# An RMSNorm kernel: the first early store on ScalarE's queue cut from four rows per partition to one, the second grown from four to seven

## The chip, the core and the metric

The kernel runs on one core of a Trainium2 chip. The core has five engines that work side by side: TensorE (PE) for matrix products, VectorE (DVE), ScalarE (ACT) and GpSimd (POOL) for elementwise work and reductions, and SyncE (SP), which here only issues DMA transfers. Transfers between the chip's memory and the 128 partitions of the on-chip memory are carried out by 16 DMA engines. SP and ACT each have a queue of their own that feeds the same 16 DMA engines: the profile calls SP's queue q1 and ACT's queue q10. The metric is the device time of one execution in microseconds (us), as the median over runs.

## The reference

```python
def reference(x, gamma):          # x: 16 x 1024 x 512 fp32, gamma: 512 fp32
    eps = 1e-5
    rms = np.sqrt(np.mean(x ** 2, axis=-1, keepdims=True) + eps)
    return (x / rms * gamma).astype(np.float32)
```

Every row of 512 numbers is divided by its root mean square and multiplied by gamma. The input is 16384 rows, 33.55 MB, and the output is as large.

## The kernel before

The 16384 rows are cut into four tiles t = 0 to 3, each of 128 partitions with 32 rows (R) of 512 fp32 numbers. One row of one partition is 2048 bytes; one row on all partitions is 256 KB, and a whole tile 8 MB. Three slots of on-chip memory hold a tile each; tile 3 uses slot 0 again, once tile 0 has been stored from it (`slot_of`, line 87).

The order of the work is written out by hand. `load` (line 44) always issues on SP's queue. `store` (line 48) issues on SP's queue unless another is named. In every transfer, a run of r rows of one partition is contiguous in both memories, so that a transfer is 128 packets of r x 2048 bytes, 8 for each of the 16 DMA engines.

The work on the engines goes by `groups` (line 76): tile, first row, number of rows, how the rows are cut for the square sums, and how many rows at the end of the group are POOL's share. For each group, ACT squares the rows and DVE sums them (`square_sums`, lines 96 and 97), ACT takes the root and DVE the reciprocal (`inverse_rms`, lines 102 and 103). Then POOL scales its share and multiplies it by gamma (lines 109 and 110), ACT scales the other rows one at a time (line 118), and DVE multiplies these by gamma in one instruction (`times_gamma`, line 122). The square sums of the next group are issued ahead of this group's scaling. All results are written in place, into the slot.

Tile 0 has three groups: rows 0 to 6 (rows 0 to 3 by ACT and DVE, rows 4 to 6 by POOL), rows 7 to 15 (7 to 10 by ACT and DVE, 11 to 15 by POOL), and rows 16 to 31. The first eight rows of tile 0 are stored from ACT's queue, in two pieces: one is issued while the group at row 7 is worked on (line 173), the other while the group at row 16 is (line 179). A third such piece is rows 0 to 3 of tile 1 (line 181). All other stores, and all loads, are issued by SP in a fixed order (`transfers`, line 129): among others the store of tile 0's rows 8 to 15 and 16 to 31, then the loads of tile 2's rows 23 to 31 and of tile 3 into slot 0. The load of tile 3's rows 0 to 15 overwrites the rows that the two pieces on ACT's queue, and the store of rows 8 to 15, have read, so SP waits for these three before it issues that load.

Of the kernel before, what the change touches and what calls it, by code (L numbers as in the profile page):

```python
# [9 lines left out]
def kernel(  # L10
# [6 lines left out]
    nc = tc.nc  # L17
# [30 lines left out]
    def store(t, slot, r0, r1, queue=nc.sync):  # L48
        dma = queue.dma_start(out=ov[t][:, r0:r1], in_=slots[slot][:, r0:r1])  # L49
        before_scale.append((slot, r0, r1, dma))  # L50
# [38 lines left out]
    def square_sums(ss, t, g, r, m, k):  # L89
        if m == 9:  # L90
            sq = slots[2][:, 23:32, :]
        else:
            home, name, most = ((psum, "sq_psum", 7), (const, "sq_sbuf", 5))[k % 2]
            sq = home.tile([P, most, D], fp32, name=name)
        rows = slots[slot_of[t]][:, g + r : g + r + m, :]
        nc.scalar.activation(out=sq[:, :m], in_=rows, func=AF.Square)  # L96
        nc.vector.tensor_reduce(  # L97
            out=ss[:, r : r + m, 0], in_=sq[:, :m], axis=mybir.AxisListType.X, op=OP.add
        )

    def inverse_rms(ss, n):
        nc.scalar.activation(out=ss[:, :n, 0], in_=ss[:, :n, 0], func=AF.Sqrt, bias=eps_t, scale=1.0 / D)  # L102
        nc.vector.reciprocal(out=ss[:, :n, 0], in_=ss[:, :n, 0])  # L103
        return ss

    def scale_by_pool(rstd, t, g, n, share):
        part = slots[slot_of[t]][:, g + n - share : g + n, :]
        by_row = rstd[:, n - share : n].to_broadcast([P, share, D])
        nc.gpsimd.tensor_tensor(out=part, in0=part, in1=by_row, op=OP.mult)  # L109
        last = nc.gpsimd.tensor_tensor(  # L110
            out=part, in0=part, in1=gamma_b.to_broadcast([P, share, D]), op=OP.mult
        )
        before_scale.append((slot_of[t], g + n - share, g + n, last))

    def scale(rstd, t, g, r0, r1):
        x = slots[slot_of[t]]
        for r in range(r0, r1):
            nc.scalar.activation(out=x[:, g + r, :], in_=x[:, g + r, :], func=AF.Copy, scale=rstd[:, r])  # L118

    def times_gamma(t, g, r0, r1):  # L120
        part = slots[slot_of[t]][:, g + r0 : g + r1, :]
        scaled = nc.vector.tensor_tensor(  # L122
            out=part, in0=part, in1=gamma_psum.to_broadcast([P, r1 - r0, D]), op=OP.mult
        )
        for slot, b0, b1, earlier in before_scale:
            if slot == slot_of[t] and b0 < g + r1 and g + r0 < b1:
                tc.declare_no_dep(scaled.ins, earlier.ins, reason="ScalarE waited for it before it scaled these rows")

    def transfers(t, g):
        if (t, g) == (0, 0):  # L130
            load(1, 1, 16, 32)
            load(2, 2, 0, 23)
        elif (t, g) == (0, 16):
            store(0, 0, 8, 16)
            store(0, 0, 16, 32)
            load(2, 2, 23, 32)
            load(3, 0, 0, 16)
            load(3, 0, 16, 32)
        elif (t, g) == (1, 16):
            store(1, 1, 4, 32)  # L140
        elif (t, g) == (2, 16):
            store(2, 2, 0, 32)
        elif (t, g) == (3, 0):
            store(3, 0, 0, 16)
        elif (t, g) == (3, 16):
            store(3, 0, 16, 32)

    def pieces_of(group):
        t, g, n, pieces, share = group
        ss = stats.tile([P, 16, 1], fp32, name="ss")  # L150
        r = 0
        todo = []
        for k, m in enumerate(pieces):
            todo.append((ss, t, g, r, m, k))
            r += m
        return ss, todo
# [6 lines left out]
    for k, group in enumerate(groups):  # L163
        t, g, n, pieces, share = group
        mine = n - share
        half = (mine + 1) // 2
        ahead = groups[k + 1 :][:1]
        ss, todo = pieces_of(ahead[0]) if ahead else (None, [])
        scale_by_pool(rstd, t, g, n, share)
        for piece in todo[:2]:  # L170
            square_sums(*piece)
        if (t, g) == (0, 7):
            store(0, 0, 0, 4, nc.scalar)
        scale(rstd, t, g, 0, half)
        for piece in todo[2:]:
            square_sums(*piece)
        scale(rstd, t, g, half, mine)
        if (t, g) == (0, 16):
            store(0, 0, 4, 8, nc.scalar)
        elif (t, g) == (2, 0):  # L180
            store(1, 1, 0, 4, nc.scalar)
        times_gamma(t, g, 0, mine)
        transfers(t, g)
        for nxt in ahead:
            rstd = inverse_rms(ss, nxt[2])
# [30 lines left out]
```

## Time and profile before

| what | value |
|---|---|
| median of 3 runs | 161.56 us (161.45 to 161.64) |
| the profiled execution | 161.69 us, its span 159.8 us |
| DVE, ACT, POOL busy | 112.0, 107.8, 106.4 us |
| moved by DMA | 67.12 MB, 420 GB/s over the span |
| packets of q1 (SP) and q10 (ACT), share of 16 engines | 93.5% and 4.7% |
| last instruction of DVE (line 122) | from 132.10, 7.09 us long |
| issue of the two pieces on ACT's queue | 27.41 and 40.02 us |

The span is what the profiler saw of the program; the execution's own time contains 1.89 us around it. A time in the trace counts from the start of the span. "q1" and "q10" are SP's and ACT's DMA queues; "SPq" and "ACTq" are the sequencers that issue on them. A DMA share of 1 means that all 16 DMA engines were busy; over short stretches it can lie above 1, because a packet is counted in the stretch in which it begins. Beside the page and its views, the trace holds a record of every DMA packet (when it began, how long it took, its size, its queue) and of every step of a semaphore by which a transfer reports that it has landed; the single packet times and landing times in this document are from these records.

### The profile page before, as it was taken

How to read it: one execution, taken by the hardware profiler on the slowest of the kernel's cores; microseconds unless marked ns; L12 is line 12 of the kernel's file. 1: busy time of each engine (PE TensorE's matmuls, PEld its weight loads, DVE VectorE, ACT ScalarE, POOL GpSimd, SP SyncE). 2: the span in 40 equal slices, each digit the busy share in tenths (PEclk: the TensorE clock that was granted, in tenths of full speed). 3: DMA queues.
4: the chain of work that ended last, by engine and by line, in shares of the span. 5: the costliest groups of instructions: out<-in, count | busy, mean ns of one | idle time of the engine just before them, and what ended most of it. 6: DMA issues, size and time to landing. Idle time of an engine off the chain costs nothing.

```text
span 159.8 us, 273 instructions
## 1 busy us (share of the span) xinstructions
PE 2.0 (1%) x2; PEld 0.5 (0%) x2; DVE 112.0 (70%) x39; ACT 107.8 (67%) x108; POOL 106.4 (67%) x24
## 2 busy tenths in 40 slices
PE   0050000000000000000000000000000000000000
PEld 0010000000000000000000000000000000000000
DVE  0019098899798999999999999999999009800000
ACT  3071966975999999999899999989970990000000
POOL 1000960994999599999999999999999990000000
DMA  5999999999999998998999999999996997999995
GB/s 179 431 427 468 443 418 410 377 449 408 455 476 443 443 410 365 423 500 370 434 468 394 470 445 390 501 459 459 459 476 279 525 476 312 394 468 451 394 435 222
DMA packets 2747, 67.12 MB, mean 420 GB/s; under 512 B 313, under 2 KB 314, under 8 KB 442
## 3 DMA queue, kind: packets, MB, share of 16 engines
q1 hardware_dynamic: 2314, 63.97, 93.5%
q10 hardware_dynamic: 432, 3.15, 4.7%
q14 instruction: 1, 0.01, 0.0%
HBM read 33.56 MB, written 33.55 MB: 420 GB/s over the span
## 4 chain that ended last, share of the span: by engine, by line
DVE 59%; ACT 21%; DMA 4%; issue 1%; ACTq 1%; SPq 0%
DVE ss L97 36%; DVE slot L122 23%; ACT slot L118 8%; ACT slot L96 8%; ACT sq_psum L96 5%; DMA slot<-in_x_dram 4%; DVE ss L103 1%; ACT ss L102 0%; ACTq L211 0%; ACT gamma_b L162 0%; SPq L45 0%; ACTq L49 0%; ACTq L96 0%
## 5 line engine op out<-in xcount | busy, mean ns | idle before, releaser
L109 POOL TENSOR_TENSOR slot<-slot,ss 128x3584 f32<-128x3584 f32 (+2 forms) x9 | 46.9, 5213 | 24.2 <-DVE ss L103 24.2
L110 POOL TENSOR_TENSOR slot<-slot,gamma_b 128x3584 f32<-128x3584 f32 (+2 forms) x9 | 59.2, 6582 | 0.7
L97 DVE TENSOR_REDUCE ss<-sq_psum 128x7 f32<-128x3584 f32 (+1 forms) x13 | 42.2, 3245 | 13.7 <-ACT sq_psum L96 13.7
L118 ACT ACTIVATE slot<-slot,ss 128x512 f32<-128x512 f32 x75 | 47.2, 706 | 4.7 <-DVE ss L103 4.7
L122 DVE TENSOR_TENSOR slot<-slot,gamma_psum 128x4608 f32<-128x4608 f32 (+2 forms) x9 | 41.3, 4589 | 8.7 <-ACT slot L118 8.7
L96 ACT ACTIVATE sq_psum<-slot 128x3584 f32<-128x3584 f32 (+1 forms) x13 | 34.5, 2657 | 6.3 <-DMA slot<-in_x_dram 5.7
L97 DVE TENSOR_REDUCE ss<-slot 128x9 f32<-128x4608 f32 x3 | 14.9, 4954 | 4.4 <-ACT slot L96 4.2
L97 DVE TENSOR_REDUCE ss<-sq_sbuf 128x5 f32<-128x2560 f32 x5 | 14.0, 2800 | 0.0
L96 ACT ACTIVATE slot<-slot 128x4608 f32<-128x4608 f32 x3 | 12.1, 4032 | 0.0
L96 ACT ACTIVATE sq_sbuf<-slot 128x2560 f32<-128x2560 f32 x5 | 11.6, 2324 | 0.3 <-DMA slot<-in_x_dram 0.3
L102 ACT ACTIVATE ss<-ss,eps_t 128x16 f32<-128x16 f32 (+2 forms) x9 | 2.7, 304 | 11.7 <-DVE ss L97 11.7
L103 DVE RECIPROCAL ss<-ss 128x16 f32<-128x16 f32 (+2 forms) x9 | 2.1, 235 | 0.4 <-ACT ss L102 0.4
L66 PE MATMUL gamma_psum<-gamma_row,ones_col 1*128 1x512 f32 x2 | 2.0, 1122 | 8.7 <-DMA gamma_row<-in_gamma_dram 8.7
L72 ACT ACT_TABLE_LOAD x1 | 1.3, 1283 | 1.2 <-PEq L200 1.2
L162 ACT COPY gamma_b<-gamma_psum 128x512 f32<-128x512 f32 x1 | 0.6, 564 | 0.0
L66 PEld LDWEIGHTS gamma_psum<-gamma_row,ones_col 1*128 1x128 f32 x2 | 0.5, 305 | 8.6 <-issue 8.6
L64 POOL MEMSET ones_col<- 1x128 f32 x1 | 0.2, 194 | 0.3 <-POOLq L200 0.3
L200 POOL MEMSET const-float32-0.0<- 128x1 f32 x1 | 0.1, 98 | 0.2 <-issue 0.2
L72 ACT ACTIVATE table<-eps_t 128x1 f32<-128x1 f32 x1 | 0.2, 202 | 0.0
L200 POOL MEMSET const-bfloat16-1.0<- 128x1 bf16 x1 | 0.1, 101 | 0.0
L200 POOL MEMSET const-uint8-127<- 128x1 uint8 x1 | 0.1, 101 | 0.0
L200 POOL MEMSET const-float32-1.0<- 128x1 f32 x1 | 0.1, 98 | 0.0
(1 smaller groups left out, 0.1 us busy)
## 6 DMA issues: line engine op xcount, KB each, us to landing
slot<-in_x_dram SPq DMA_DIRECT2D x5, 4096.0 KB, 25.0
out_dram<-slot SPq DMA_DIRECT2D x3, 4096.0 KB, 20.2
out_dram<-slot SPq DMA_DIRECT2D x1, 7168.0 KB
slot<-in_x_dram SPq DMA_DIRECT2D x1, 5888.0 KB
out_dram<-slot ACTq DMA_DIRECT2D x3, 1024.0 KB
slot<-in_x_dram SPq DMA_DIRECT2D x1, 2304.0 KB, 25.7
slot<-in_x_dram SPq DMA_DIRECT2D x1, 2048.0 KB, 10.0
out_dram<-slot SPq DMA_DIRECT2D x1, 2048.0 KB
```

Of the source, the lines that this page charges most:

```text
L66: nc.tensor.matmul(gamma_psum[:, 0], ones_col, gamma_row, start=True, stop=True)
L72: nc.scalar.activation(out=table, in_=eps_t, func=AF.Sqrt)
L96: nc.scalar.activation(out=sq[:, :m], in_=rows, func=AF.Square)
L97: nc.vector.tensor_reduce(out=ss[:, r : r + m, 0], in_=sq[:, :m], axis=mybir.AxisListType.X, op=OP.add)
L102: nc.scalar.activation(out=ss[:, :n, 0], in_=ss[:, :n, 0], func=AF.Sqrt, bias=eps_t, scale=1.0 / D)
L103: nc.vector.reciprocal(out=ss[:, :n, 0], in_=ss[:, :n, 0])
L109: nc.gpsimd.tensor_tensor(out=part, in0=part, in1=by_row, op=OP.mult)
L110: last = nc.gpsimd.tensor_tensor(out=part, in0=part, in1=gamma_b.to_broadcast([P, share, D]), op=OP.mult)
L118: nc.scalar.activation(out=x[:, g + r, :], in_=x[:, g + r, :], func=AF.Copy, scale=rstd[:, r])
L122: scaled = nc.vector.tensor_tensor(out=part, in0=part, in1=gamma_psum.to_broadcast([P, r1 - r0, D]), op=OP.mult)
L162: nc.scalar.copy(out=gamma_b[:, 0], in_=gamma_psum[:, 0])
L200: nc = _bacc.Bacc("TRN2", target_bir_lowering=False, num_devices=1)
```

## The change

The first piece on ACT's queue is row 0 of tile 0 instead of rows 0 to 3. The second is rows 1 to 7 instead of rows 4 to 7. The places in the program at which they are issued stay the same.

```diff
         if (t, g) == (0, 7):
-            store(0, 0, 0, 4, nc.scalar)
+            store(0, 0, 0, 1, nc.scalar)
         scale(rstd, t, g, 0, half)
         for piece in todo[2:]:
             square_sums(*piece)
         scale(rstd, t, g, half, mine)
         if (t, g) == (0, 16):
-            store(0, 0, 4, 8, nc.scalar)
+            store(0, 0, 1, 8, nc.scalar)
         elif (t, g) == (2, 0):
             store(1, 1, 0, 4, nc.scalar)
```

## The prediction

> **What bounds the kernel now.** I read the page's head and its DMA rows first, then the chain that ended last, then a table of busy times by stretch, then the waits of SP's queue, then the timeline around the two stores. The page first:
>
> ```profile
> span 159.8 us, 273 instructions
> ...
> DMA  5999999999999998998999999999996997999995
> ...
> q1 hardware_dynamic: 2314, 63.97, 93.5%
> q10 hardware_dynamic: 432, 3.15, 4.7%
> ```
>
> The two queues' packets take 93.5% + 4.7% = 98.2% of the time of 16 DMA engines: 0.982 x 159.8 = 156.9 us. In the packet records the first packet of the kernel's loads begins at 1.76 us and the last one ends at 158.56. 1.76 + 156.8 = 158.6, so from the first packet to the last there is no gap on the DMA engines. The rest is the last landing (158.92), 0.8 us to the end of the span, and 1.9 us around it.
>
> The chain of waits seems to say something else. Its end:
>
> ```profile
> 125.95 6.13 ACT slot L118 x10
> 132.08 0.02 issue
> 132.10 7.09 DVE slot L122
> ```
>
> It follows the engines to 139.2 us, where DVE's last instruction ends, and stops there. But the last store, issued then, has its first packet at 148.35: 9.1 us behind older packets in q1. A queue that is empty needs about 1.0 us from issue to packet (SP's first issue at 0.74, first packet at 1.76). So the engines could be some 8.1 us later (148.35 - 1.0 - 139.2) before a DMA engine ran dry. The engines don't set the end; the packets do. The table by stretch (columns: stretch, its length, busy time of PE, PEld, DVE, ACT, POOL, clock, DMA share, GB/s):
>
> ```profile
> 4.00:20.00 16.00, 2.04 (x2) 0.49 (x2) 4.09 (x2) 7.67 (x4) 3.82 (x2) 1.00 1.04 445
> 20.00:28.00 8.00, 0.00 (x0) 0.00 (x0) 7.27 (x3) 5.43 (x7) 2.78 (x2) 1.00 0.97 418
> 28.00:34.00 6.00, 0.00 (x0) 0.00 (x0) 5.32 (x2) 6.00 (x5) 5.92 (x2) 1.00 0.95 371
> 34.00:44.00 10.00, 0.00 (x0) 0.00 (x0) 8.93 (x4) 7.43 (x5) 7.77 (x2) 1.00 1.03 442
> 44.00:62.00 18.00, 0.00 (x0) 0.00 (x0) 17.37 (x7) 17.64 (x21) 16.22 (x4) 1.00 1.00 429
> 62.00:90.00 28.00, 0.00 (x0) 0.00 (x0) 28.00 (x12) 26.45 (x28) 27.84 (x5) 1.00 1.01 436
> 104.00:139.20 35.20, 0.00 (x0) 0.00 (x0) 27.05 (x9) 22.14 (x29) 27.68 (x5) 1.00 1.01 436
> 139.20:150.00 10.80, 0.00 (x0) 0.00 (x0) 0.00 (x0) 0.00 (x0) 0.00 (x0) 1.00 1.00 434
> ```
>
> The DMA share is about 1 everywhere, at 418 to 445 GB/s, except from 28 to 34 us: busy, but 371 GB/s. There the packets are stretched: 31 packets of 32 KB that begin between 29.0 and 31.3 take up to 1.687 us instead of 1.213, together 0.52 us for each engine. It is the one loss in the middle of the run.
>
> **The change, part by part.** These lines of the timeline are the two issues and what stands around them, and the first reader of the load that the second store runs beside:
>
> ```profile
> 25.10 2.28 DVE L122 TENSOR_TENSOR slot<-slot,gamma_psum 128x2048 f32<-128x2048 f32 x1
> 27.41 0.38 ACTq L49 DMA_DIRECT2D out_dram<-slot  x1
> 40.02 0.34 ACTq L49 DMA_DIRECT2D out_dram<-slot  x1
> 64.45 3.14 ACT L96 ACTIVATE sq_psum<-slot 128x3584 f32<-128x3584 f32 x1
> ```
>
> *The issues.* The first store waits for DVE's one instruction over rows 0 to 3 (25.10 + 2.28 = 27.38), and row 0 alone needs the same instruction. The second waits for POOL's rows 4 to 6 and for row 7, which DVE ends at 39.72; rows 1 to 3 are ready since 27.38. Both are still 128 packets, so I take 0.38 and 0.34 us of ACTq for the issues as before. No issue moves: 0.
>
> *The packets, one engine's eight of each store.* In the records an 8192-byte packet of q10 takes 0.309 us, a 14336-byte one (first seen as a load of seven rows) 0.535, a 2048-byte one (the load of row 0) 0.084. First store: 8 x 0.309 = 2.47 us before, 8 x 0.084 = 0.67 after, 1.80 less. Second: 2.47 before, 8 x 0.535 = 4.28 after, 1.81 more. Sum: +0.01 us. Since the DMA engines have no gap, all of it would be on the path. The durations are of loads; no store of these sizes is shown. Bounds for a 2048-byte store packet: below, the bytes alone at the slope between 8192 and 32768 bytes ((1.213 - 0.309) / 24576 x 2048 = 0.075 us, a gain of 0.07 us for eight); above, the longest 2048-byte packet of the run, 0.667 us at its start (4.7 us for eight). For 14336 bytes: 0.527 by the same slope below (-0.06 us), 0.998 above (+3.7 us). I take the medians, 0.084 and 0.535, because the line through 8192 and 32768 bytes goes through both, and because 8192-byte stores lie on the line of the loads.
>
> *A rule against it.* The Trainium skill, "DMA: Bandwidth & Descriptors", section Bandwidth, advises transfers of at least 1 MiB, since each carries about 2.0 us that don't grow with its size; the first store falls to 256 KB. By its fit (2.0 us + bytes / 436 GB/s, given for another issue path) an estimate is 2.6 + 6.2 us for the new pair against 4.4 + 4.4 for the old, the same sum. Here nothing waits for that fixed part: between issue and first packet of the first store (27.8 to 31.98 us) the engines move loads.
>
> *The loads beside them.* Packets of the two queues alternate one by one: the first store's groups come every 1.515 us (1.213 + 0.309). With smaller packets in between, the load of tile 1's rows 16 to 31 lands 1.8 us sooner (45.3 to about 43.5); its reader starts at 50.49 behind DVE, so nothing is gained. The load of tile 2's rows 0 to 22 then starts 1.8 us sooner, has 1.8 us more of store packets between its own, and lands where it did, 61.3; its reader, the last line above, starts at 64.45 and has 3.1 us to spare. From there on q1 stands where it stood before: 0.
>
> *Who waits for the stores.* SP's own waits:
>
> ```profile
> SPq L45 <- DMA out_dram<-slot: 19.5, 3, 9.5
> SPq L211 <- DMA out_dram<-slot: 19.1, 2, 9.6
> ```
>
> The load of tile 3's rows 0 to 15 waits for both pieces and for the store of rows 8 to 15. The last landing is that store's, at 66.2. The second piece landed at 59.6; with 1.8 us more it lands near 61.4, 4.8 us before SP could go on. Behind SP's wait stand the load of rows 16 to 31 and the later stores, and q1 then holds packets until about 81. On ACT one wait moves: in tile 3 the scaling of row 1, not of row 4, now checks the second piece, at 97 us; it passed long ago: 0.
>
> *Sum.* +0.01 us on the profiled 161.69 us, which lies 0.13 above the median of 161.56. Forecast: 161.57 us.
>
> **Rivals.**
>
> *Faster: the loss at 29 to 32 us shrinks with the first store.* The stretched packets begin 1.2 us after the first store's issue ends and stop as its packets begin. If the loss is work done for that store by its bytes, a quarter of the bytes leaves a quarter of 0.52 us: -0.39, so 161.18 us; at most -0.52, 161.05. Against it: no packet of the store runs then, the second and third store of the same size (40.02 and 86.70) show nothing of the kind, and the first loads of q1 were stretched likewise (0.6 us for each engine from 1.8 to 7 us). That looks like the first use of a queue, whatever its size. 128 packets are set up either way.
>
> *Slower: the new packets cost what they did at the start of the run.* There, the 2048-byte packets took 0.117 us on average, the 14336-byte ones 0.572. If such packets don't follow on each other at full rate when they change places with long loads, 8 x 0.033 + 8 x 0.037 = 0.56 us come on top: 162.13 us. It decides from about 0.32 us, that is, 0.040 us for each of the eight small packets alone. For it: nothing in the run shows short store packets between long loads. Against it: the 8192-byte ones in that place cost 0.309 throughout, nothing over the line.
>
> *Slower: the second store lands too late.* SP would have to be held up from 66.3 until past some 80 us before q1 ran dry; the store would have to land 18 us later than I work out. Then each further microsecond is one on the time, 162.6 for one. Nothing speaks for it.
>
> *Faster by earlier loads.* That needs an engine that waits for the load which lands at 45.3 and an end set by the engines; neither is so. It gives 161.57, the forecast.
>
> **How the numbers follow.** The forecast, with the rival that gives the same time, has 0.64. The lost stretch shrinking has 0.14, and 0.02 goes to gains in the same place that I can't name: faster 0.16. The dearer packets have 0.17, the late second store or another hold-up of the queue 0.03: slower 0.20. Within 0.2% (0.32 us, about what a measurement of this kernel can tell from no change) is 161.24 to 161.88. The range goes down to the shrunken loss, 161.15, and up past the dearer packets, 162.2; it leaves out a loss that vanishes whole and a price of packets nearer to its upper bound, together about 0.12. The forecast's own range is 161.4 to 161.75, the runs' spread and a little more.
>
> **What would show it.** Right: q10's packets in two groups, eight per engine of about 0.084 us from about 32 us and eight of about 0.535 from about 44 us; DMA share near 1 from 2 to 158 us; the same dip at 28 to 34 us; tile 1's second load landing near 43.5; all instructions from 64 us on where they were. Wrong: a dip that is gone or smaller (the first rival), packets of q10 or the loads between them that take longer than these medians (the second), a gap in q1 (the third). The forecast fails where the time of the packets depends on their order and not only on their number and size.

## The result: slower, and scattered

| | before | changed |
|---|---|---|
| median of 8 runs | 161.61 us (161.45 to 161.78) | 162.63 us (161.94 to 163.59) |
| ratio | | 1.0063, 95% interval 1.0040 to 1.0086 |
| the profiled execution | 161.69 us, span 159.8 | 163.59 us, span 161.7 |

The changed kernel is slower by 0.6%, outside the forecast range, and its runs lie 1.65 us apart where those of the kernel before lie 0.33 apart. (A ratio here is not the quotient of the two medians beside it; with scattered runs the two differ by up to 0.3%.) The profiled execution of the changed kernel is the slowest of its eight, so that it shows the loss large.

The head and the DMA rows of the changed kernel's page:

```profile
span 161.7 us, 273 instructions
...
DMA  5999999999979979999999989999799969899990
...
q1 hardware_dynamic: 2314, 63.97, 92.5%
q10 hardware_dynamic: 432, 3.15, 4.6%
```

(92.5% + 4.6%) of 161.7 us is 157.0 us of packets, where the kernel before had 156.9. The average engine has no more to do, and 1.9 us of the span are new. The table by stretch shows where they are (columns as in the prediction; the last two are DMA share and GB/s). The kernel before, at the old dip and at its end:

```profile
28.00:34.00 6.00, 0.00 (x0) 0.00 (x0) 5.32 (x2) 6.00 (x5) 5.92 (x2) 1.00 0.95 371
40.00:52.00 12.00, 0.00 (x0) 0.00 (x0) 10.42 (x3) 12.00 (x13) 11.92 (x2) 1.00 1.06 457
56.00:60.00 4.00, 0.00 (x0) 0.00 (x0) 4.00 (x2) 3.64 (x6) 4.00 (x1) 1.00 0.95 410
158.00:159.00 1.00, 0.00 (x0) 0.00 (x0) 0.00 (x0) 0.00 (x0) 0.00 (x0) 1.00 0.01 0
159.00:160.00 1.00, 0.00 (x0) 0.00 (x0) 0.00 (x0) 0.00 (x0) 0.00 (x0) 1.00 0.00 0
```

The changed kernel, the same stretches:

```profile
28.00:34.00 6.00, 0.00 (x0) 0.00 (x0) 5.56 (x2) 6.00 (x5) 5.92 (x2) 1.00 0.98 421
40.00:52.00 12.00, 0.00 (x0) 0.00 (x0) 10.67 (x3) 12.00 (x13) 11.92 (x2) 1.00 1.04 433
56.00:60.00 4.00, 0.00 (x0) 0.00 (x0) 4.00 (x2) 3.64 (x6) 4.00 (x1) 1.00 0.89 367
158.00:159.00 1.00, 0.00 (x0) 0.00 (x0) 0.00 (x0) 0.00 (x0) 0.00 (x0) 1.00 0.08 33
159.00:160.00 1.00, 0.00 (x0) 0.00 (x0) 0.00 (x0) 0.00 (x0) 0.00 (x0) 1.00 0.08 33
```

Two things are to be seen. First, the dip at 28 to 34 us is gone (371 to 421 GB/s), and slower stretches have come at 40 to 52 and 56 to 60 us instead. By the packet records, the excess of all packets over the straight line of size between 24 and 60 us is 0.55 us for each engine before and 0.59 after: the loss moved and kept its size. In the profiles of all the kernels below this sum lies between 0.49 and 0.75 us, whatever the pieces; only its place changes. Second, from 158 to 160 us the changed kernel shows a DMA share of 0.08 and 33 GB/s: that is about one engine of 16, with one 32 KB packet in each microsecond. In the packet records, 15 of the 16 engines end between 158.01 and 158.61 us, where all 16 ended before (158.03 to 158.56). The last one ends at 160.50. In this profile, this engine alone is the 1.9 us.

When it fell behind is written in the landings. A transfer has landed when all 16 engines have done their share; the last engine comes after the median one by 0.28 us in the landing at 66.3 us, then by 0.58 (76.5), 1.08 (82.2), 1.44 (92.7) and 2.22 (105.2), and by as much to the end. Four packets lie on these steps: a 32 KB store packet at 74.1 us that took 2.09 us instead of 1.21, an 18 KB load packet at 76.2 (0.91 instead of 0.69), and 32 KB load packets at 90.7 (1.34) and 101.4 (2.29). The other packets of these sizes at 74 and 76 us took the usual time to 0.01 us. The records don't name the engine of a packet, so that these four are one engine's follows from the times alone. The lag stays to the end: no other engine takes over a part of the late engine's packets.

On the engines' side the delay shows above all as this wait. The kernel before:

```profile
ACT sq_sbuf L96 <- DMA slot<-in_x_dram: 0.3, 1, 0.3
```

The changed kernel:

```profile
ACT sq_sbuf L96 <- DMA slot<-in_x_dram: 1.3, 1, 1.3
```

It isn't the price: DVE's last instruction starts at 132.62 instead of 132.10 us, and the last store's packets begin at 148.4 in both.

### The profile page after: what moved, and what is told of

The parts are those of the page before. It is cut to its first block, busy times and chain, and to the rows that moved or that the text cites. A ratio compares the mean times of both kernels' runs of the same rounds, so it can differ in the third digit from the quotient of the medians.

```text
span 161.7 us, 273 instructions
## 1 busy us (share of the span) xinstructions
PE 2.0 (1%) x2; PEld 0.5 (0%) x2; DVE 112.2 (69%) x39; ACT 107.7 (67%) x108; POOL 106.4 (66%) x24
## 3 DMA queue, kind: packets, MB, share of 16 engines
q1 hardware_dynamic: 2314, 63.97, 92.5%
## 4 chain that ended last, share of the span: by engine, by line
DVE 36%; ACT 27%; DMA 21%; issue 1%; ACTq 1%; SPq 0%
DMA slot<-in_x_dram 21%; DVE ss L97 19%; DVE slot L122 17%; ACT slot L118 11%; ACT slot L96 7%; ACT sq_psum L96 6%; ACT sq_sbuf L96 1%; ACT ss L102 0%; ACTq L211 0%; DVE ss L103 0%; ACT gamma_b L162 0%; SPq L45 0%; SPq L49 0%; ACTq L49 0%; ACTq L96 0%
```

## The experiments

All ratios are to the kernel before, run beside on the same chip. "Dip" is the excess of the packets that begin from 28 to 34 us over the straight line of size, in us for each engine. Each dip comes from the one execution that was profiled. None of the runs of the kernel before that stood beside these was above 162.43 us, so runs of 163 us and more are counted. The experiments ran on four chips: the first four kernels of the table on one, two_six, no_first, four_singles and after_moved on a second, few_parts, before_moved and the two oneway kernels on a third, the two with `nudge` on a fourth. The changed kernel itself was not run beside the kernels on the third and the fourth.

| kernel | first store, then second | median (range), us | ratio (95%) | dip | runs from 163 us |
|---|---|---|---|---|---|
| changed, again | 1 row, 7 rows | 163.28 (161.63 to 164.06) | 1.0078 (1.0050 to 1.0105) | 0 | 8 of 12 |
| small_first | 1, 4 (3 by SP) | 162.10 (161.71 to 163.41) | 1.0041 (1.0018 to 1.0064) | 0 | 3 of 12 |
| large_second | 4, 7 | 161.79 (161.56 to 162.40) | 1.0005 (0.9992 to 1.0019) | 0.42 | 0 of 12 |
| swap | 7, 1 | 162.14 (161.74 to 162.61) | 1.0025 (1.0012 to 1.0037) | 0.74 | 0 of 12 |
| two_six | 2, 6 | 161.79 (161.48 to 163.36) | 1.0020 (1.0001 to 1.0039) | 0.06 | 1 of 12 |
| no_first | none, 8 | 162.72 (162.57 to 164.18) | 1.0096 (1.0066 to 1.0125) | 0 | 2 of 6 |
| four_singles | 4 x 1 row, 4 | 164.56 (164.48 to 164.73) | 1.0184 (1.0171 to 1.0197) | 0.02 | 4 of 4 |
| few_parts | 4 rows of 32 partitions, the rest | 161.95 (161.72 to 162.37) | 1.0026 (1.0017 to 1.0034) | 0.37 | 0 of 11 |
| after_moved | 1, 7, other order on q1 | 162.58 (161.71 to 164.06) | 1.0068 (1.0037 to 1.0100) | 0 | 6 of 12 |
| before_moved | 4, 4, other order on q1 | 162.03 (161.72 to 162.36) | 1.0027 (1.0017 to 1.0038) | 0.56 | 0 of 11 |
| oneway_before | 4, 4, no late loads | 161.46 (161.30 to 161.89) | 0.9991 (0.9980 to 1.0002) | 0.40 | 0 of 11 |
| oneway_after | 1, 7, no late loads | 161.46 (161.33 to 161.70) | 0.9991 (0.9982 to 1.0000) | 0 | 0 of 11 |
| after_nudge | 8 KB packets, then 1, 7 | 163.85 (163.12 to 164.46) | 1.0140 (1.0116 to 1.0164) | 0.25 | 6 of 6 |
| no_first_nudge | 8 KB packets, then none, 8 | 162.67 (162.04 to 163.99) | 1.0073 (1.0046 to 1.0100) | 0.26 | 4 of 12 |

### Which of the two pieces: the changed kernel again, and each part alone

The changed kernel again, without an edit:

> The changed kernel a second time, to see which part of its profile comes back. Theory A (the seven-row packets of the second store slow the loads they change places with): again about 1.006 of the kernel before, with stretched packets of the load of tile 2's rows 0 to 22 between 42 and 59 us, together about 0.4 us for each of the 16 DMA engines. Theory B (the small first store): the same time, and the dip at 29 to 32 us gone again. Theory C (one DMA engine falls behind the other 15 by chance, at places far from the two stores): fifteen engines end near 158.5 us again and one later, but the long packets of that one lie elsewhere than at 74 and 101 us, and the lag is 0.5 to 2 us.

The first piece alone:

```diff
-            store(0, 0, 0, 4, nc.scalar)
+            store(0, 0, 0, 1, nc.scalar)
...
         elif (t, g) == (0, 16):
+            store(0, 0, 1, 4)
             store(0, 0, 8, 16)
```

> Only the first piece made small: row 0 on ScalarE's queue, rows 1 to 3 go to SyncE's queue ahead of rows 8 to 15, and the second piece stays rows 4 to 7. Theory A: no loss, 0.998 to 1.001 of the kernel before. Theory B: the loss stays, 1.004 to 1.009. Theory C doesn't say which piece matters: a scatter of runs of 0.5 us or more if the small piece is what lets one engine fall behind, 0.2 us if not.

The second piece alone:

```diff
-            store(0, 0, 8, 16)
+            store(0, 0, 11, 16)
...
-            store(0, 0, 4, 8, nc.scalar)
+            store(0, 0, 4, 11, nc.scalar)
```

> Only the second piece made large: the first stays rows 0 to 3, the second is rows 4 to 10, and SyncE's store begins at row 11. Theory A: the loss is there, 1.004 to 1.009, with stretched load packets between 44 and 60 us. Theory B: 0.999 to 1.001, with the dip at 29 to 32 us as before the change. Theory C: a scatter of runs of 0.5 us or more if the large piece is what lets one engine fall behind.

The sizes the other way round:

```diff
-            store(0, 0, 0, 4, nc.scalar)
+            store(0, 0, 0, 7, nc.scalar)
...
-            store(0, 0, 4, 8, nc.scalar)
+            store(0, 0, 7, 8, nc.scalar)
```

> The sizes the other way round: first piece rows 0 to 6, second row 7. Theory A (the large piece costs where it stands beside loads): a loss between 32 and 46 us, 1.003 to 1.009. Theory B (a small first piece costs): no loss, 0.999 to 1.001, or a gain. Theory C: one late engine only if unequal pieces as such bring it, 1.003 to 1.01.

Measured: the loss and the scatter came back in the changed kernel. In this profile four engines were late, not one: twelve end by 158.75 us, the others at 159.70, 159.81, 160.14 and 160.16. The end of the span shows them, with a DMA share of 0.31 after 158 us, where the kernel before had 0.01:

```profile
156.00:158.00 2.00, 0.00 (x0) 0.00 (x0) 0.00 (x0) 0.00 (x0) 0.00 (x0) 1.00 0.99 426
158.00:159.00 1.00, 0.00 (x0) 0.00 (x0) 0.00 (x0) 0.00 (x0) 0.00 (x0) 1.00 0.31 131
```

Their long packets began at 74.1 to 74.3, 76.2 to 76.3, 89.0 to 89.5 and 101.3 to 101.9 us: the number of late engines changed from run to run, the places did not. So theory C's "by chance" holds for which engines and how many, and is wrong for where.

The large second store alone costs nothing that can be measured (+0.05%, interval from -0.08 to +0.19); theory A falls. The stretched loads that it forecast between 42 and 59 us did come in the changed kernel (0.64 us for each engine in this profile), but they came in place of the dip and not on top of it. The small first store alone costs 0.41%, with three runs at 163 us. The first piece is the one that matters. The changed kernel's 0.78% with the large second behind it is higher, but the two intervals overlap, so that the second makes it worse is likely and not shown. In the profile of small_first, itself a quick run of 161.97 us, no engine is late. The swapped sizes cost 0.25% with no run over 162.61; their dip has grown to 0.74 us from 0.52, and that 0.22 us is half of the 0.46 between the medians. Theory A had put that loss at 0.3 to 0.9%, between 32 and 46 us; it is smaller and stands earlier, before the large piece's first packets. Theory B had no loss here, which is wrong too.

### Small packets or few bytes: no first store, four single rows, two rows, 32 partitions

No first store:

```diff
-        if (t, g) == (0, 7):
-            store(0, 0, 0, 4, nc.scalar)
...
-            store(0, 0, 4, 8, nc.scalar)
+            store(0, 0, 0, 8, nc.scalar)
```

> The first piece is left out and rows 0 to 7 go out together at the place of the second. There are no 2 KB packets. Theory D (short packets between long loads put the DMA engines out of step): no loss, 0.998 to 1.002 of the kernel before, and no engine later than the others. Theory E (what counts is when the bytes run: few stored at 31 to 42 us, many from 43 us on): the loss of the changed kernel or more, 1.005 to 1.012, with one or a few engines 0.8 to 2.3 us behind.

Four rows in four stores:

```diff
-            store(0, 0, 0, 4, nc.scalar)
+            for r in range(4):
+                store(0, 0, r, r + 1, nc.scalar)
```

> The first piece keeps its four rows, but as four stores of one row each: 2 KB packets, 32 for each engine, in place of eight of 8 KB. The second piece is rows 4 to 7 as before the change. Theory D: the loss is there or larger, 1.004 to 1.015. Theory E: no loss, 0.999 to 1.002; 0.2 us may come from three more issues and 24 more short packets for each engine (24 x 0.009 us).

Two rows and six:

```diff
-            store(0, 0, 0, 4, nc.scalar)
+            store(0, 0, 0, 2, nc.scalar)
...
-            store(0, 0, 4, 8, nc.scalar)
+            store(0, 0, 2, 8, nc.scalar)
```

> Half way: rows 0 and 1 first, then rows 2 to 7. Theory D: less than the changed kernel, 1.000 to 1.003, since the packets are 4 KB. Theory E: between the two kernels, 1.001 to 1.005, with some of the runs at 163 us and the others at 161.7.

Few bytes in large packets:

```diff
-            store(0, 0, 0, 4, nc.scalar)
+            before_scale.append((0, 0, 4, nc.scalar.dma_start(out=ov[0][0:32, 0:4], in_=slots[0][0:32, 0:4])))
...
+            before_scale.append((0, 0, 4, nc.scalar.dma_start(out=ov[0][32:P, 0:4], in_=slots[0][32:P, 0:4])))
             store(0, 0, 4, 8, nc.scalar)
```

> The first store carries as few bytes as in the changed kernel (256 KB), but in 8 KB packets: rows 0 to 3 of partitions 0 to 31, two packets for each engine. The other 96 partitions' rows 0 to 3 and then rows 4 to 7 follow at the place of the second, all in 8 KB packets. Theory D (2 KB packets are what hurts): no loss, 0.999 to 1.001. Theory E (few bytes stored early is what hurts): the loss, 1.003 to 1.01, some runs at 163 us or more, and no dip at 28 to 32 us.

Measured: without a 2 KB packet on ACT's queue, no_first lost 0.96%. Short packets aren't needed for the loss, so theory D falls as the whole story. But theory E had one or a few engines late, and in the profile of no_first (162.59 us) all 16 are: they end within 0.5 us of each other, from 158.70 to 159.23, and their packets from 62 to 150 us hold 0.85 us of excess for each engine (0.02 in the kernel before). Some 50 long packets, at 74, 75 to 78 and 88 to 90 us, share it. So the long packets at these places can also hit all engines alike. few_parts stored as few bytes early as the changed kernel and lost 0.26%, at the low end of what theory E said or under it; no run was over 162.37, and the dip was there. In its profile (162.28 us) one engine is late as well, but from another place: 0.6 us behind in the landing at 33.3 us, beside the dip, and 0.9 at the end. So few early bytes alone didn't bring the scatter; but the changed kernel was not run beside few_parts, so that this rests on another chip's scatter. two_six lies between the two kernels, as theory E has it, and within what theory D said as well.

four_singles didn't tell D from E, because it costs something else. Packets of the two queues alternate one by one (the profile calls each run of one partition a packet). With 32 short packets for each engine instead of eight, the four rows needed 32 turns with the loads, one every 1.30 us beside 32 KB loads and one every 1.82 beside 46 KB ones, and their last packets began at 70.9 us (39.8 in the changed kernel). Rows 4 to 7 went behind them, on the same queue, until 80 us. SP's load of tile 3 waits for these. The chain of waits of this kernel:

```profile
39.92 41.08 DMA out_dram<-slot
81.00 0.02 issue
81.02 13.51 DMA slot<-in_x_dram
```

41 us from the issue of rows 4 to 7 to their landing, then the load. q1 ran dry meanwhile: the packet records have 1.1 us of idle time for each engine between 80 and 84 us, and under 0.05 us from 5 to 150 us in the kernel before. That is not the whole of the 2.9 us: another 1.2 us for each engine are long packets of tile 3's loads, at 82 us (the first behind the gap) and 88 to 92 us, on nearly all engines. The dry stretch is the prediction's rival of a second store that lands too late, in a kernel that brings it about. The Trainium skill, "DMA: Bandwidth & Descriptors", section Queues, rings and completion order, says that an engine takes turns between queues by packets that typically hold 9 to 17 descriptors. Here the trace differs: each turn was a single run of one partition, 32 turns for the 32 short runs of each engine.

### Does it need the change of direction on q1: other order, and no late loads

The changed kernel and the kernel before, each with this edit:

```diff
-            store(0, 0, 16, 32)
             load(2, 2, 23, 32)
+            store(0, 0, 16, 32)
```

> The changed kernel with SyncE's load of tile 2's rows 23 to 31 ahead of its store of tile 0's rows 16 to 31, so that the change from stores to loads on q1 that lay at 75 us lies at about 66 and 82 us, and the change from loads to stores at about 71. Theory F (the late engine loses its time where q1 changes direction): the long packets of single engines move from 74 and 76 us to within 2 us of these places. If they come by the clock or by the work of the engines, they stay at 74 and 76 us. The time: between 161.5 and 164 us by either.

> The kernel before with SyncE's load of tile 2's rows 23 to 31 ahead of its store of tile 0's rows 16 to 31, to stand beside the changed kernel with the same order. Theory E: the old pieces keep the engines together in this order too, 161.4 to 161.9 us and runs within 0.4 us of each other, so that the changed pieces cost 0.5 to 1 us here as well. If the loss hangs on where exactly q1 changes direction, this one scatters from 161.7 to 164 us like the changed kernel in this order.

Both kernels with no loads after 61 us:

```diff
-            load(2, 2, 23, 32)
-            load(3, 0, 0, 16)
-            load(3, 0, 16, 32)
+            away(0, 2, 23, 32)
+            away(1, 0, 0, 16)
+            away(1, 0, 16, 32)
```

`away` is a store on SP's queue of the same rows to a spare tensor; it enters the same list as `store`. These two kernels never load tile 3 and the last nine rows of tile 2, and work on what the slots hold. They leave out more than a change of direction: SP no longer waits for the two pieces on ACT's queue, so that it has issued the three transfers by 57.1 us instead of 76.9.

> The kernel before without a change of direction on q1 after 61 us: the loads of tile 2's rows 23 to 31 and of tile 3 are replaced by stores of the same rows, of the same size, to a spare tensor, so that the computation of tile 3 and of those rows runs on what the slots hold. By theory F (single engines lose time where q1 changes direction) and by the prediction: within 0.5 us of the kernel before, runs within 0.3 us of each other.

> The same with the changed kernel's two pieces: loads after 61 us replaced by stores of the same size to a spare tensor. Theory F: the loss is gone, within 0.2 us of the run above (which has the old pieces), no run over 0.5 us beyond the fastest, no long packets of single engines after 62 us. If the late engines come from the two stores themselves, or by the clock: 0.7 to 1.5 us above the run above, with long packets near 74 and 101 us as in the changed kernel.

Measured: in the other order, the long packets left 74 and 76 us. In after_moved they stood at 68.9 to 70.6, among the last load packets before q1 turns to stores, and at 101.1 to 101.9, where loads end in both orders; before_moved had a few at 70.5, 79.7 and 101.5 too, with an excess of up to 0.19 us. The work of DVE, ACT and POOL starts at the same times in after_moved as in the changed kernel, to 0.02 us up to 78 us, and the long packets moved by some 4 us; so they aren't set by that work. The scatter is the changed pieces' again: 161.71 to 164.06 us against 161.72 to 162.36, on two chips.

Without late loads there is no loss: 161.46 us with the old pieces and 161.46 with the new, no run over 161.89, no long packet after 62 us in either profile. The end of oneway_after's span:

```profile
56.00:60.00 4.00, 0.00 (x0) 0.00 (x0) 4.00 (x2) 3.64 (x6) 4.00 (x1) 1.00 0.86 352
158.00:159.00 1.00, 0.00 (x0) 0.00 (x0) 0.00 (x0) 0.00 (x0) 0.00 (x0) 1.00 0.01 0
159.00:161.50 2.50, 0.00 (x0) 0.00 (x0) 0.00 (x0) 0.00 (x0) 0.00 (x0) 1.00 0.00 0
```

The slower stretch at 56 to 60 us is there, and no engine is late. (That stretch isn't the large second store's own: the packet records have 0.57 us of excess there in small_first, and none in large_second.) So the two stores by themselves, with all that they do to the loads before 61 us, cost nothing here. This is as theory F has it, and in both orders most of the long packets stood where q1 changes direction. But the run doesn't single out the change of direction: it takes away the late loads themselves and SP's wait along with it. And the changed kernel was not run beside these two; that it would have lost time on their chip is not shown, though before_moved, on the same chip and with the loads, has a few long packets.

### Is the dip a protection?

Until here, every kernel with a dip of 0.37 us or more had no run of 163 us, and of those without one all but oneway_after (and four_singles, for its own reason) had some. So 8 KB packets, two for each engine, were put on ACT's queue at the place of the first store, in two kernels that lack the dip. In the changed kernel they stand ahead of its first store:

```diff
+    def nudge():
+        dma = nc.scalar.dma_start(out=spare[0:32, 0:4], in_=slots[0][0:32, 0:4])
+        before_scale.append((0, 0, 4, dma))
...
         if (t, g) == (0, 7):
+            nudge()
             store(0, 0, 0, 1, nc.scalar)
```

> The changed kernel with one transfer more, right ahead of its first store: rows 0 to 3 of 32 partitions to a spare tensor, two packets of 8 KB for each engine (0.62 us of DMA time). Theory G (what the changed kernel lacks is the early large packets on ScalarE's queue, which stretch the loads at 28 to 32 us and after which no engine falls far behind): 162.1 to 162.6 us, the dip at 28 to 34 us back with some 0.4 us for each engine, and no run over 163 us. If the dip is only a companion: the extra 0.62 us come on top of the changed kernel's times, 162.4 to 164.5 us, a median of about 163.5 with some runs over 163.5, dip or no dip.

> The kernel without a first store (rows 0 to 7 together at the place of the second, 162.57 to 164.18 us) with the same extra transfer at the place of the first: two packets of 8 KB for each engine to a spare tensor. Theory G: 162.1 to 162.6 us, lower than without the extra transfer in spite of its 0.62 us, with the dip back. If the dip is only a companion: 163.2 to 164.8 us.

Measured: a smaller dip came in both (0.25 and 0.26 us), and the late engines stayed. after_nudge's six runs lie from 163.12 to 164.46 us, as forecast for a dip that is only a companion; in the profile of no_first_nudge one engine ends at 161.02 us, one at 159.46 and the others by 158.91. But no_first_nudge's median, 162.67 us, lies between the two forecasts: five of its twelve runs lie from 162.04 to 162.10 us, where no_first's fastest was 162.57, in spite of 0.62 us of packets more (on another chip), and the excess from 62 to 150 us in its profile is 0.16 us for each engine against 0.85. So a dip of 0.25 us doesn't keep single engines from falling behind, and theory G fails as it was put. Whether a full dip of 0.37 us or more would, these two runs don't tell, and in no_first the extra packets seem to have helped.

## Why the prediction was wrong, point by point

- **What bounds the kernel** was read rightly as far as it went: packets without a gap from 1.76 us on, engines with time to spare. But "the packets set the end" was worked out for the average of 16 engines. The end is set by the last engine, and the average doesn't show it. The 16 engines of the kernel before ended within 0.5 us of each other, and I took that for granted.
- **The step that failed** is the sum of the packets: eight of each store at the medians, all of it on the path, +0.01 us, and nothing else. Its terms for the two stores were exact: all 128 small packets of q10 took 0.084 us and all 128 of the seven-row store 0.535. What failed is the term for all that comes later, "from there on q1 stands where it stood before: 0". The loss, some 0.6 to 0.8%, is in other transfers' packets, 30 to 58 us after the second store had begun, on one engine in the profiled execution (four packets, 2.3 us too long together, 1.9 us on the span) and on four in the next. The last sentence of the prediction named this condition (the time may depend on the packets' order) and I gave it no mechanism and no chance of its own.
- **The dip**: I kept it as it was, because I read it as the first use of a queue. That was wrong: the first use is still there and the dip isn't. The rival said that it goes by the bytes. That is wrong too: 256 KB in 8 KB packets brought 0.37 us (few_parts; 0.25 and 0.26 with `nudge`), 512 KB in 4 KB packets 0.06 (two_six), 256 KB in 2 KB packets none. It goes with the packets' size more than with the bytes, up to 0.74 us at 14 KB. The rival's gain came, 0.52 us, and was paid back at once beside the second store, so that the average engine had nothing from it.
- **The dearer packets**, the rival on the slower side, didn't happen as put: the new store packets cost their medians. Its price, 162.13 us, still lies below the measured median; with it as the range's end, the slower side was cut too short.
- **The late second store** was rightly called no danger here (landings at 61.7 us for it and 61.4 for the load beside it; I had 61.4 and 61.3), and four_singles shows what it costs when it comes true. (The landings of the kernel before in the prediction are 0.1 to 0.2 us early: 45.3, 59.6, 61.3 and 66.2 are 45.5, 59.7, 61.5 and 66.4 when all 16 engines are counted.)
- **The rule of transfers of at least 1 MiB**, which the prediction takes from the Trainium skill, "DMA: Bandwidth & Descriptors", section Bandwidth (the fixed 2.0 us and the fit stand in its section Anatomy of one DMA), pointed the right way for the small first piece, but not by its mechanism: a fixed cost would have been on these transfers, and their packets took no longer than forecast. And no_first, with one store of 2 MB, was no faster (162.72 us).
- **What stays open**: why a small or absent first store brings long packets near later changes of direction, on one engine, on a few or on all. It is shown that the first piece matters and the second alone doesn't, that 2 KB packets aren't needed, that a dip of 0.25 us doesn't protect, and that there is no loss without later loads, as far as two kernels show it beside which the changed kernel was not run. Whether the change of direction or something else that goes with these loads does it was not separated. What of an engine's state carries from 31 to 60 us over to 74 and 101 us can't be seen in these records, which don't name the engine of a packet; no run here tells it.

## What to carry to other kernels

Where DMA engines are full from end to end, add up the packets, but then ask for the last engine as well as for the mean: look at the final microseconds of the span (a share near 1/16 is one late engine) and at how far the last of the 16 comes behind the median in each landing. Here a smaller transfer on a second queue changed later transfers that don't touch its rows; runs that scatter were the first sign, so compare several before one profile is explained. And count the packets, not the bytes, of a store that takes turns with another queue: in four_singles each one waited for one packet of the other.

## What was not expected of the hardware

- One DMA engine fell 2 us behind the other 15 through four packets, each up to 1.07 us too long, and stayed behind to the end of the program. In the two profiles of the changed kernel the places repeat (74, 76, 89 to 91, 101 us), the number of late engines doesn't (one, then four). In no_first all 16 were hit.
- Most of the long packets stand just ahead of a change of direction: the last stores before loads (74 us), the last loads before stores (28 to 32, 68.9 to 70.6, 89 to 90, 101 us; in small_first, two_six and few_parts also 56 to 58), up to three microseconds before the first packet of the new direction. Others stand just behind one: 76 us, and 82 us in four_singles. With stores only, after 61 us, there were none.
- Two queues took turns packet by packet at every size tried, 2 KB against 46 KB included: 1 MB in 2 KB runs held back what was queued behind it by more than 30 us (four_singles).
